# Sums of weight blocks moved from VectorE to GpSimd, and seven block products in ten gate and up units

## The chip, the cores and the metric

The kernel runs on one core of a Trainium2 chip. The metric is the device time of one execution in microseconds. Engines: TensorE (PE) multiplies matrices, VectorE (DVE) and ScalarE (ACT) work element by element, GpSimd (POOL) likewise, SyncE (SP) issues the loads.

## What is computed

One decoder layer on 256 tokens of width 2048, in fp32: a convolution group and an attention group, their mix, and a gated feed-forward network. The change is in the network alone:

```python
hf = rmsnorm(x, pre_ffn_norm[l])
ff = (jax.nn.silu(hf @ w_gate[l]) * (hf @ w_up[l])) @ w_down[l]
x = x + rmsnorm(ff, post_ffn_norm[l])
```

`w_gate` and `w_up` are 2048 x 5632, `w_down` is 5632 x 2048.

## The kernel before, in words

**Precision.** Every fp32 operand is split into two fp16 halves, and a product of two operands is three matmuls: high by high (L739), high by low (L740), low by high (L741). Activations are split once. Weights arrive as fp32 in a staging tile `st` (128 x 2048, 1 MB), ScalarE writes the high half `whi` (L694), VectorE the low half `wlo` from `st` and `whi` (L695).

**Pairs and units.** Weights are cut into pairs. A pair is two tiles of 128 rows by two groups of 512 columns, four blocks of 128 x 512 side by side in one staging tile. With two tiles of 128 tokens that is a product of 2 x 2 blocks by 2 x 2 blocks. `Unit.plain_all` does it with eight block products (24 matmuls). `Unit.fast` does it with seven (21 matmuls), from four further blocks that are sums of the weight blocks and from sums of the activation blocks. A gate and up unit is eight pairs and gives 512 gate and 512 up columns; there are eleven, `u` from 0 to 10. Of a gate and up unit's 512-column group half is gate and half is up; `swiglu` (L796, L806, and splits by L109) makes the network's hidden activations from it. Down has two units of 22 pairs, ten of them fast, in an order that alternates plain and fast and ends with two plain ones.

**A fast pair's weights.** `Feed.blocks` loads the pair, splits its first 1536 columns (three of the blocks) and then writes three sums over the staging tile in place, on VectorE at L709: one instruction of 2 x 512 columns and two of 512. `Feed.get` then splits all 2048 columns a second time, now of the four sums. A plain pair is split once, 2048 wide.

**What a fast unit adds at its end.** Four products have accumulators of their own in PSUM. After the last fast pair a ScalarE copy (L768), four adds on VectorE (L770 to L773) and four more in `block` (L782) put them together. Each of the eight adds has one input in PSUM. `hf_sums` (L669) makes the sums of the activations for gate and up in unit 0, `swiglu` those for down.

**What sets the order.** The program is written in the order in which TensorE uses the pairs: `get` issues pair `k` and pair `k + 1`. A scheduler then orders each engine's queue by that priority and by when inputs are ready, and inside the feed `chain` keeps an engine's instructions in the order written. Buffers limit how far it runs ahead: four staging tiles, eight `whi` and eight `wlo`. Each engine works off its queue strictly in order.

Of the kernel before, what the change touches and what calls it, by code (L numbers as in the profile page):

```python
# [10 lines left out]
F16 = mybir.dt.float16  # L11
F32 = mybir.dt.float32
I32 = mybir.dt.int32
AF = mybir.ActivationFunctionType
ALU = mybir.AluOpType
AX = mybir.AxisListType

P = 128
# [20 lines left out]

FAST = tuple(range(0, 20, 2))  # L40
NU = NG // 2
GU_UNITS = (1, 3, 5, 7, 9)
GU_FAST = 5
EPS = 1e-6
QK_SCALE = float((NOPE + ROPE) ** -0.5)
NEG = -1.0e30
# [14 lines left out]
def hymba_layer(ctx: ExitStack, tc: tile.TileContext, x, xT, pos, inv_freq, g_pre, w_in, w_lat,  # L61
                q_norm, w_uqn, w_uqp, kv_norm, w_uk, w_uv, conv_w, conv_v, g_attn,
                w_out, g_post, g_ffn, w_gu, w_dn, g_ffo, out):
    nc = tc.nc

    const = ctx.enter_context(tc.tile_pool(name="const", bufs=1))
    stage = ctx.enter_context(tc.tile_pool(name="stage", bufs=4))
    wsp = ctx.enter_context(tc.tile_pool(name="wsp", bufs=8))
    work = ctx.enter_context(tc.tile_pool(name="work", bufs=2))
    small = ctx.enter_context(tc.tile_pool(name="small", bufs=4))  # L70
# [3 lines left out]

    BF16 = mybir.dt.bfloat16
    KB = 256
    arena = const.tile([P, 82 * KB], F32, name="arena")

    def region(kb, shape, dtype=F32):

        n = int(np.prod(shape)) * (2 if dtype == F16 else 4) // 4
        a = int(kb * KB)
        v = arena[:, a : a + n]
        if dtype != F32:
            v = v.bitcast(dtype)
        names = "abcd"[: len(shape)]
        if len(shape) > 1:
            v = v.rearrange(f"p ({' '.join(names)}) -> p {' '.join(names)}", **dict(zip(names[:-1], shape[:-1])))
        return v
# [3 lines left out]
    def nm(base):  # L93
        uid[0] += 1
        return f"{base}_{uid[0]}"
# [20 lines left out]
    class Weights:  # L116


        def __init__(self, kt, n):
            self.kt, self.n = kt, n  # L120
            self.kpb = max(1, 2048 // n)
            self.parts = []
# [484 lines left out]
    for tb in range(NTB):  # L607
        ss4 = smalls(4)
        for j in range(4):
# [3 lines left out]
            m = mix[:, tb, cs]  # L613
# [31 lines left out]
    aw = region(44, (8, P))  # L645
    hw4 = region(48, (2, 4, P), F16)
    hw3 = region(50, (2, 3, P), F16)
    hS = region(70, (3, 16, P), F16)

    def a_of(k, tb):  # L650
        return aT[:, k // 2, 4 * tb + k % 2, :], aT[:, k // 2, 4 * tb + 2 + k % 2, :]
# [7 lines left out]
    def hf_fast(i):  # L659
        s = [(hS[:, i // 2, 2 * b + i % 2, :], hS[:, i // 2, 8 + 2 * b + i % 2, :]) for b in range(4)]  # L660
        return [hf_of(2 * i + 1, 1), hf_of(2 * i, 0), hf_of(2 * i + 1, 0), s[0], s[1], s[2], s[3]]

    def hf_sums(c):

        g0, g1 = [sized(tb, c).rearrange("p (i k t) -> p i k t", i=2, k=2) for tb in range(NTB)]
        sm = region(44, (4, 2, P))
        for d, p, m in ((0, g1[:, :, 0], g1[:, :, 1]), (1, g0[:, :, 0], g1[:, :, 0]),
                        (2, g0[:, :, 0], sm[:, 0]), (3, g0[:, :, 1], sm[:, 2])):
            nc.vector.tensor_tensor(sm[:, d], p, m, op=ALU.subtract)  # L669
        hl = region(48, (2, 8 * P), F16)  # L670
        split(hl[:, 0, :], hl[:, 1, :], sm.rearrange("p s i t -> p (s i t)"), X_S)
        nc.sync.dma_start_transpose(hS[:, c], hl.rearrange("p a n -> p (a n)"))

    class Feed:

        def __init__(self, pairs):
            self.pairs = pairs  # L680
            self.parts = {}
            self.st = {}
            self.last = {}

        def chain(self, engine, ins):
# [13 lines left out]
        def blocks(self, k):  # L699

            src, scale, fast = self.pairs[k]
            st = stage.tile([P, 2048], F32, tag="stage", name=nm("st")).rearrange("p (b n) -> p b n", b=4)
            nc.sync.dma_start(st, src)
            self.parts[k] = self.split(st, 1536 if fast else 2048, scale)
            if fast:
                b12 = st[:, 3:4, :].to_broadcast([P, 2, 512])
                for d, p, m in ((st[:, 0:4:3, :], st[:, 0:2, :], b12), (st[:, 1, :], st[:, 0, :], st[:, 1, :]),
                                (st[:, 2, :], st[:, 1, :], st[:, 2, :])):
                    self.chain("DVE", nc.vector.tensor_tensor(d, p, m, op=ALU.add))  # L709
                self.st[k] = st  # L710

        def get(self, k, ahead=1):
            for n in range(k, min(k + ahead + 1, len(self.pairs))):
                if n not in self.parts:
                    self.blocks(n)
            parts = self.parts[k]
            if k in self.st:
                parts = parts + self.split(self.st.pop(k), 2048, self.pairs[k][1])
            return parts

    class Unit:

# [31 lines left out]
        def fast(self, blocks, w, last):  # L754
            if self.sums is None:
                self.sums = [self.other() for _ in range(4)]
            X, Y, Z, Q = self.sums
            A22, A11, A12, S1, S3, S2, S4 = blocks
            self.mm(self.E[0][0], (0, 0), A12, w[2])
            self.mm(self.E[0][1], (0, 1), S4, w[1])  # L760
            self.mm(X, "X", A11, w[0], last)
            self.mm(Y, "Y", S2, w[4], last)
            self.mm(Z, "Z", S3, w[6], last)
            self.mm(Q, "Q", S1, w[3], last)
            self.mm(self.E[1][0], (1, 0), A22, w[5])
            if last:
                xs_ = work.tile([P, 512], F32, tag="hl", name=nm("xs"))
                nc.scalar.copy(xs_, X)  # L768
                m, n_, q2 = [work.tile([P, 512], F32, tag="ss", name=nm(b), bufs=3) for b in ("m", "n", "q2")]
                nc.vector.tensor_tensor(m, xs_, Y, op=ALU.subtract)  # L770
                nc.vector.tensor_tensor(n_, m, Z, op=ALU.add)
                nc.vector.tensor_tensor(m, Q, m, op=ALU.subtract)
                nc.vector.tensor_tensor(q2, Q, n_, op=ALU.subtract)  # L773
                self.fix = [[xs_, m], [n_, q2]]
# [10 lines left out]
    def swiglu(j, unit, c):  # L785
# [19 lines left out]
        for d, p, m in ((4, 0, 1), (5, 2, 0), (6, 2, 4), (7, 3, 6)):  # L805
# [5 lines left out]


    KP = KD // 2
    gu_order = [GU_FAST, 0, 1, GU_FAST + 1] + list(range(2, GU_FAST)) + list(range(GU_FAST + 2, KP))
    gu_orders = [gu_order if u in GU_UNITS else list(range(KP)) for u in range(NU)]

    slow = [i for i in range(NG) if i not in FAST]
    order = [i for f, p in zip(FAST, slow) for i in (p, f)] + slow[len(FAST) :]
    feed = Feed([(w_gu[u, i], W_S, u in GU_UNITS and i < GU_FAST) for u in range(NU) for i in gu_orders[u]]
                + [(w_dn[u, i], WD_S, i in FAST) for u in range(2) for i in order])  # L820
    for u in range(NU):
        unit = Unit(hf_of)
        if u == 0:
            ws = [feed.get(i, 0) for i in range(KP)]
            for tb in range(NTB):
# [3 lines left out]
                if tb == 0:  # L829
                    for c in range((GU_FAST + 1) // 2):  # L830
                        hf_sums(c)
        else:
            for n, i in enumerate(gu_orders[u]):
                w = feed.get(u * KP + n)
                if u in GU_UNITS and i < GU_FAST:
                    unit.fast(hf_fast(i), w, i == GU_FAST - 1)
                else:
# [150 lines left out]
```

## Time and profile before

| | |
|---|---|
| median of three runs | 1000.91 us (1000.34 to 1001.33) |
| the profiled execution | 1001.55 us |
| its span from the first to the last instruction | 999.7 us |
| TensorE busy | 959.6 us, 96% |
| VectorE busy | 876.3 us, 88% |
| ScalarE busy | 578.1 us, 58% |
| GpSimd busy | 33.6 us, 3% |
| gate and up: first matmul, then down | from 326 us; from 776 to 989 us |

The profiled execution is one run of the program with the hardware's profiler on; its span leaves out 1.85 us around the instructions. Busy time of TensorE counts overlapping matmuls once, so 96% says that it rarely stood still, not that it could do no more. Names such as `wlo<-st,whi` read: output from inputs. Times in rows are microseconds from the start of the span, "mean ns" are nanoseconds.

### The profile page before, as it was taken

What the parts mean: (1) busy time and instruction counts of PE and PEld (TensorE: products, weight loads), DVE (VectorE), ACT (ScalarE), POOL (GpSimd) and SP (SyncE); (2) the same over time, 40 slices, a digit from 0 to 9 for tenths busy, and PEclk for the clock granted to TensorE, in tenths of its full rate; (3) what the DMA queues carried; (4) which work ended last, traced back from release to release, by engine and by line L of the source; (5) the groups of instructions that cost most, each with busy time, mean ns of one, the idle gap of its engine ahead of it and who ended that gap; (6) DMA issues with size and microseconds to landing.
All of it is one profiled execution on the core that took longest, in us unless ns stands there. A gap on an engine that the chain in (4) does not pass through costs nothing.

```text
span 999.7 us, 11980 instructions
## 1 busy us (share of the span) xinstructions
PE 959.6 (96%) x4577; PEld 454.4 (45%) x4577; DVE 876.3 (88%) x1024; ACT 578.1 (58%) x632; POOL 33.6 (3%) x50
## 2 busy tenths in 40 slices
PE   6999997999899998999999999999999999999995
PEld 2444553775444443444444444444444444444442
DVE  6799999999967999989898997897996988899855
ACT  7796764664666555655656645654663565555521
POOL 0000000033100100000000000000000000000000
PEclk9999998999999999999999999999999999999998
DMA  8974656476654966776875874784686646645532
GB/s 340 346 262 126 243 197 192 154 247 211 211 210 118 325 167 197 256 278 197 320 214 178 317 236 155 272 288 156 220 309 234 218 185 246 238 175 220 210 127 85
DMA packets 84010, 221.95 MB, mean 222 GB/s; under 512 B 55792, under 2 KB 56432, under 8 KB 61424
## 3 DMA queue, kind: packets, MB, share of 16 engines
q1 hardware_dynamic: 83232, 220.26, 63.7%
q10 hardware_dynamic: 720, 0.93, 0.3%
q8 instruction: 36, 0.59, 0.2%
q14 instruction: 22, 0.18, 0.1%
HBM read 204.25 MB, written 4.19 MB: 209 GB/s over the span
## 4 chain that ended last, share of the span: by engine, by line
PE 60%; DVE 23%; issue 5%; ACT 4%; DMA 3%; POOL 1%; SPq 0%; DVEq 0%; POOLq 0%; ACTq 0%
PE acc L740 10%; PE acc L741 10%; PE acc L739 10%; PE tmp L741 6%; PE tmp L740 6%; PE tmp L739 6%; DVE wlo L695 6%; DVE arena L289 3%; DVE wlo L109 3%; DVE st L709 2%; PE acc L155 2%; PE acc L153 2%; PE acc L154 2%; DMA st<-in_w_gu 2%; POOL sm L207 1%
## 5 line engine op out<-in xcount | busy, mean ns | idle before, releaser
L694 ACT ACTIVATE whi<-st 128x2048 f16<-128x2048 f32 (+1 forms) x177 | 317.1, 1798 | 228.7 <-PE acc L741 77.6
L695 DVE SCALAR_TENSOR_TENSOR wlo<-st,whi 128x2048 f16<-128x2048 f32 (+1 forms) x177 | 375.2, 2150 | 52.9 <-ACT whi L694 52.5
L740 PE MATMUL acc<-wlo,arena 128*128 128x512 f16 x620 | 235.0, 379 | 4.7 <-DVE wlo L695 4.7
L739 PE MATMUL acc<-whi,arena 128*128 128x512 f16 x620 | 235.0, 379 | 2.5 <-DVE q L773 1.4
L741 PE MATMUL acc<-whi,arena 128*128 128x512 f16 x620 | 235.0, 379 | 0.0
L153 PE MATMUL acc<-whi,arena 128*128 128x512 f16 (+1 forms) x380 | 143.5, 378 | 5.5 <-ACT whi L108 5.5
L741 PEld LDWEIGHTS <-arena 128*128 128x128 f16 x951 | 93.0, 98 | 117.4 <-issue 5.6
L154 PE MATMUL acc<-wlo,arena 128*128 128x512 f16 (+1 forms) x380 | 143.4, 377 | 2.2 <-DVE wlo L109 2.0
L740 PEld LDWEIGHTS <-arena 128*128 128x128 f16 x951 | 93.0, 98 | 114.3 <-issue 2.4
L739 PEld LDWEIGHTS <-arena 128*128 128x128 f16 x951 | 93.0, 98 | 113.3 <-DVE a L796 1.2
L155 PE MATMUL acc<-whi,arena 128*128 128x512 f16 (+1 forms) x380 | 143.3, 378 | 0.0
L739 PE MATMUL tmp<-whi,arena 128*128 128x512 f16 x331 | 125.4, 379 | 0.0
L740 PE MATMUL tmp<-wlo,arena 128*128 128x512 f16 x331 | 125.4, 379 | 0.0
L741 PE MATMUL tmp<-whi,arena 128*128 128x512 f16 x331 | 125.4, 379 | 0.0
L109 DVE SCALAR_TENSOR_TENSOR wlo<-st,whi 128x2048 f16<-128x2048 f32 (+4 forms) x59 | 118.2, 2009 | 6.5 <-ACT whi L108 6.5
L709 DVE TENSOR_TENSOR st<-st 128x1024 f32<-128x1024 f32 x135 | 117.2, 868 | 4.1
L108 ACT ACTIVATE whi<-st 128x2048 f16<-128x2048 f32 (+4 forms) x59 | 98.5, 1677 | 34.4 <-PE acc L155 10.3
L289 DVE SCALAR_TENSOR_TENSOR arena<-arena 128x256 f32<-128x256 f32 x184 | 78.5, 488 | 0.0
L153 PEld LDWEIGHTS <-arena 128*128 128x128 f16 x380 | 37.8, 99 | 47.4 <-ACT arena L113 5.0
L155 PEld LDWEIGHTS <-arena 128*128 128x128 f16 x380 | 37.8, 99 | 44.8 <-issue 5.1
L154 PEld LDWEIGHTS <-arena 128*128 128x128 f16 x380 | 37.6, 99 | 42.3 <-issue 2.8
L295 ACT ACTIVATE x_sb<-arena 128x256 f32<-128x256 f32 x56 | 25.3, 506 | 10.1 <-DVE arena L297 10.1
(209 smaller groups left out, 667.9 us busy)
## 6 DMA issues: line engine op xcount, KB each, us to landing
st<-in_w_gu SPq DMA_DIRECT2D x88, 1024.0 KB, 5.5
st<-in_w_dn SPq DMA_DIRECT2D x44, 1024.0 KB, 5.0
st<-in_w_out SPq DMA_DIRECT2D x16, 1024.0 KB, 5.1
st<-in_w_in SPq DMA_DIRECT2D x14, 1024.0 KB, 9.2
st<-in_w_lat SPq DMA_DIRECT2D x12, 896.0 KB, 5.5
x_sb<-in_x SPq DMA_DIRECT2D x4, 1024.0 KB, 8.6
st<-in_w_uqn SPq DMA_DIRECT2D x4, 768.0 KB, 4.9
st<-in_w_uv SPq DMA_DIRECT2D x2, 1024.0 KB, 5.9
```

The costliest lines, as they stand in the source:

```text
L108: nc.scalar.activation(hi, src, AF.Copy, scale=scale)
L109: nc.vector.scalar_tensor_tensor(lo, src, scale, hi, op0=ALU.mult, op1=ALU.subtract)
L153: nc.tensor.matmul(p_ap, xh, wh, start=(start and k == 0), stop=False)
L154: nc.tensor.matmul(p_ap, xh, wl, start=False, stop=False)
L155: nc.tensor.matmul(p_ap, xl, wh, start=False, stop=(stop and k == wgt.kt - 1))
L289: nc.vector.scalar_tensor_tensor(cacc[:, cb, :], upad[:, cb, k : k + S], cw[:, cb, k : k + 1], cacc[:, cb, :], op0=ALU.mult, op1=ALU.add)
L694: self.chain("ACT", nc.scalar.activation(hi[:, :n], src, AF.Copy, scale=scale))
L695: self.chain("DVE", nc.vector.scalar_tensor_tensor(lo[:, :n], src, scale, hi[:, :n], op0=ALU.mult, op1=ALU.subtract))
L709: self.chain("DVE", nc.vector.tensor_tensor(d, p, m, op=ALU.add))
L739: nc.tensor.matmul(ps, ah, bh, start=key not in self.begun, stop=False)
L740: nc.tensor.matmul(ps, ah, bl, start=False, stop=False)
L741: nc.tensor.matmul(ps, al, bh, start=False, stop=last)
```

## The change

The three sums of a fast pair go from VectorE to GpSimd. Fast pairs are now in gate and up units 1 to 10 instead of 1, 3, 5, 7 and 9, four in each instead of five: 40 instead of 25. Down keeps its 20. A fifth staging tile is added, for which the arena gives up 6 KB per partition; two groups of activation sums are made instead of three. The feed issues up to four pairs ahead instead of one, and the second splits one pair ahead.

```diff
-GU_UNITS = (1, 3, 5, 7, 9)
-GU_FAST = 5
+GU_UNITS = tuple(range(1, NU))
+GU_FAST = 4
+
+AHEAD, AHEAD_T = 4, 1
...
-    stage = ctx.enter_context(tc.tile_pool(name="stage", bufs=4))
+    stage = ctx.enter_context(tc.tile_pool(name="stage", bufs=5))
...
-    arena = const.tile([P, 82 * KB], F32, name="arena")
+    arena = const.tile([P, 76 * KB], F32, name="arena")
...
-    hS = region(70, (3, 16, P), F16)
+    hS = region(68, (2, 16, P), F16)
...
-            self.parts = {}
-            self.st = {}
+            self.parts, self.sums, self.st = {}, {}, {}
...
-                    self.chain("DVE", nc.vector.tensor_tensor(d, p, m, op=ALU.add))
+                    self.chain("POOL", nc.gpsimd.tensor_tensor(d, p, m, op=ALU.add))
                 self.st[k] = st
 
-        def get(self, k, ahead=1):
+        def get(self, k, ahead=AHEAD):
             for n in range(k, min(k + ahead + 1, len(self.pairs))):
                 if n not in self.parts:
                     self.blocks(n)
-            parts = self.parts[k]
-            if k in self.st:
-                parts = parts + self.split(self.st.pop(k), 2048, self.pairs[k][1])
-            return parts
+            for n in range(k, min(k + AHEAD_T + 1, len(self.pairs))):
+                if n in self.st:
+                    self.sums[n] = self.split(self.st.pop(n), 2048, self.pairs[n][1])
+            return self.parts[k] + self.sums.get(k, [])
...
-    gu_order = [GU_FAST, 0, 1, GU_FAST + 1] + list(range(2, GU_FAST)) + list(range(GU_FAST + 2, KP))
+    gu_order = [4, 0, 5, 1, 6, 2, 3, 7]
```

VectorE's queue before, at the first two fast pairs of a gate and up unit (`st` is a staging tile, its number the tile's own):

```order
L695 SCALAR_TENSOR_TENSOR wlo_3861<-st_3858,whi_3860 128x1536
L709 TENSOR_TENSOR st_3858<-st_3858 128x2x512
L709 TENSOR_TENSOR st_3858<-st_3858 128x512 x2
L695 SCALAR_TENSOR_TENSOR wlo_3894<-st_3891,whi_3893 128x1536
L709 TENSOR_TENSOR st_3891<-st_3891 128x2x512
L709 TENSOR_TENSOR st_3891<-st_3891 128x512 x2
L695 SCALAR_TENSOR_TENSOR wlo_3901<-st_3858,whi_3900 128x2048
```

Each first split is followed by its three sums. VectorE's queue after the change, over the middle of a gate and up unit:

```order
L695 SCALAR_TENSOR_TENSOR wlo_4039<-st_3934,whi_4038 128x2048
L695 SCALAR_TENSOR_TENSOR wlo_4069<-st_4066,whi_4068 128x1536
L695 SCALAR_TENSOR_TENSOR wlo_4076<-st_3968,whi_4075 128x2048
L695 SCALAR_TENSOR_TENSOR wlo_4103<-st_4100,whi_4102 128x2048
L695 SCALAR_TENSOR_TENSOR wlo_4139<-st_4136,whi_4138 128x1536
L695 SCALAR_TENSOR_TENSOR wlo_4212<-st_4209,whi_4211 128x2048
L770 TENSOR_TENSOR m_4129<-xs_4127,acc_3944 128x512
L695 SCALAR_TENSOR_TENSOR wlo_4216<-st_4066,whi_4215 128x2048
```

The sums are gone from it, and a tile's second split (of `st_4066`) stands six rows behind its first. GpSimd's queue after the change, for the tiles of the same unit:

```order
L709 TENSOR_TENSOR st_3934<-st_3934 128x512 x2
L709 TENSOR_TENSOR st_3968<-st_3968 128x2x512
L709 TENSOR_TENSOR st_3968<-st_3968 128x512 x2
L709 TENSOR_TENSOR st_4066<-st_4066 128x2x512
L709 TENSOR_TENSOR st_4066<-st_4066 128x512 x2
L709 TENSOR_TENSOR st_4136<-st_4136 128x2x512
```

Sixty such triples stand there, one behind the other, with nothing else between them.

## Rows read from the trace of the kernel before

**Rows 1.** The page, busy time, share and instructions of each engine.
```profile
PE 959.6 (96%) x4577; PEld 454.4 (45%) x4577; DVE 876.3 (88%) x1024; ACT 578.1 (58%) x632; POOL 33.6 (3%) x50
```

**Rows 2.** Busy time by stretch, gate, up and down; the first line names the columns.
```profile
core 0: us, PE busy (x) PEld busy (x) DVE busy (x) ACT busy (x) POOL busy (x), PEclk, DMA share, GB/s
...
370.00:408.00 38.00, 34.79 (x161) 15.47 (x159) 36.39 (x35) 21.30 (x18) 0.00 (x0) 1.00 0.66 211
408.00:449.00 41.00, 41.00 (x192) 18.57 (x191) 36.16 (x37) 24.28 (x22) 0.00 (x0) 1.00 0.75 263
...
609.00:776.00 167.00, 167.00 (x776) 75.73 (x774) 145.08 (x144) 94.94 (x84) 0.00 (x0) 1.00 0.67 233
776.00:883.00 107.00, 107.00 (x498) 48.48 (x497) 95.83 (x72) 58.61 (x41) 0.00 (x0) 1.00 0.57 208
...
326.00:989.00 663.00, 655.73 (x3036) 296.71 (x3034) 586.76 (x545) 360.25 (x299) 4.04 (x3) 1.00 0.65 224
```

**Rows 3.** TensorE's waits: for whom, us in total, times, longest.
```profile
PE tmp L385 <- DVE kp L384: 6.2, 1, 6.2
...
PE acc L740 <- DVE wlo L695: 4.7, 3, 2.2
```

**Rows 4.** Timeline of GpSimd, attention: start, us, line, operation, tiles, count.
```profile
226.32 0.73 POOL L500 TENSOR_TENSOR arena<-arena,sq 128x256 f32<-128x256 f32 x1 [3.63 <-ACT sq L496]
...
232.65 0.75 POOL L500 TENSOR_TENSOR arena<-arena,sq 128x256 f32<-128x256 f32 x1 [4.34 <-ACT sq L496]
...
240.23 1.81 POOL L500 TENSOR_TENSOR arena<-arena,sq 128x256 f32<-128x256 f32 x1 [2.66 <-ACT sq L496]
...
245.98 0.82 POOL L500 TENSOR_TENSOR arena<-arena,sq 128x256 f32<-128x256 f32 x1 [2.70 <-ACT sq L496]
```

**Rows 5.** Timeline of VectorE at the same moments, and three conv adds at 200.92.
```profile
200.92 1.27 DVE L289 SCALAR_TENSOR_TENSOR arena<-arena 128x256 f32<-128x256 f32 x3
...
226.57 0.48 DVE L114 SCALAR_TENSOR_TENSOR arena<-tmp,gat,arena 128x256 f16<-128x256 f32 x1 [1.22 <-ACT arena L113]
...
232.72 2.82 DVE L109 SCALAR_TENSOR_TENSOR wlo<-st,whi 128x2048 f16<-128x2048 f32 x1
...
239.17 2.28 DVE L109 SCALAR_TENSOR_TENSOR wlo<-st,whi 128x2048 f16<-128x2048 f32 x1
241.37 0.47 DVE L114 SCALAR_TENSOR_TENSOR arena<-tmp,gat,arena 128x256 f16<-128x256 f32 x1
...
245.35 2.53 DVE L289 SCALAR_TENSOR_TENSOR arena<-arena 128x256 f32<-128x256 f32 x5
```

**Rows 6.** Timeline of VectorE, the fix-ups and `swiglu` of gate and up unit 1.
```profile
410.34 0.68 DVE L770 TENSOR_TENSOR m<-xs,acc 128x512 f32<-128x512 f32 x1
...
417.40 2.28 DVE L695 SCALAR_TENSOR_TENSOR wlo<-st,whi 128x2048 f16<-128x2048 f32 x1
419.60 1.15 DVE L109 SCALAR_TENSOR_TENSOR arena<-arena 128x512 f16<-128x512 f32 x2
...
421.40 2.28 DVE L695 SCALAR_TENSOR_TENSOR wlo<-st,whi 128x2048 f16<-128x2048 f32 x1
423.60 0.42 DVE L109 SCALAR_TENSOR_TENSOR ahl<-a,ahl 128x256 f16<-128x256 f32 x1
```

**Rows 7.** Groups by line and shape, the first split of fast pairs; busy, mean ns.
```profile
L695 DVE SCALAR_TENSOR_TENSOR wlo<-st,whi 128x1536 f16<-128x1536 f32 x45 | 78.8, 1751 | 10.6 <-ACT whi L694 10.6
```

**Rows 8.** Timeline of VectorE, down: three sums, then the splits behind them.
```profile
788.90 2.68 DVE L709 TENSOR_TENSOR st<-st 128x1024 f32<-128x1024 f32 x3
791.50 6.16 DVE L695 SCALAR_TENSOR_TENSOR wlo<-st,whi 128x2048 f16<-128x2048 f32 x3
```

**Rows 9.** Loads: count, KB each, median us from issue to landing.
```profile
st<-in_w_gu SPq DMA_DIRECT2D x88, 1024.0 KB, 5.5
```

**Rows 10.** Busy time by stretch, behind TensorE's wait of 6.2 us (columns as in rows 2).
```profile
160.00:170.00 10.00, 7.37 (x22) 3.08 (x23) 8.87 (x26) 5.67 (x11) 1.17 (x2) 0.66 0.51 135
```

## Prediction

> **What bounds the kernel now.** Read four views in this order. First the page's engine totals [rows 1]: TensorE is busy for 96% of the span and VectorE for 88%, so two engines stand close to the end, and the question is which of them sets it in the part that is edited. Second, the busy time by stretch [rows 2], cut at the edges of the gate and up units. Between 326 and 989 us TensorE runs for 655.73 of 663 us; in the 167 us from 609 to 776 it issues 776 matmuls, one each 0.215 us, with no gap. The same rows give VectorE's load: 36.39 of 38 us in a unit with fast pairs (370 to 408), 36.16 of 41 in the plain unit after it, 145.08 of 167 further on, 95.83 of 107 in the first half of the down projection. ScalarE has 360.25 of 663, GpSimd 4.04. Third, TensorE's waits [rows 3]: the largest in this part is for a low half that VectorE writes, 4.7 us in 3 waits. So **TensorE bounds gate, up and down, VectorE follows some 10% behind it**, and GpSimd is free. Fourth, since the change loads GpSimd, GpSimd and VectorE side by side in the attention part, the only place where both work on SBUF at once [rows 4, 5].
>
> **The change part by part.**
>
> *Matmuls.* A pair is 24 matmuls plain and 21 fast. Five units of 5 fast and 3 plain pairs (177) and six plain units (192) were 2037; ten units of 4 and 4 (180) and one plain unit are 1992. That is 45 fewer, at 0.215 us each 9.7 us of TensorE time. It is a gain only if TensorE still sets the pace. A unit then needs 180 x 0.215 = 38.7 us of TensorE.
>
> *Splits and fix-ups on VectorE.* There are 40 fast pairs in gate and up instead of 25, and each needs a second split. A 2048-wide split starts the next instruction after 2.20 us (417.40 to 419.60 in [rows 6]), a 1536-wide one after 1.75 - 0.08 = 1.67 us ([rows 7]; 0.08 is the overlap that the 2048 form has, 2.28 busy against 2.20). So each new unit has 8 x 2.20 + 4 x 1.67 = 24.3 us of splits. The eight fix-up adds and the gate's own work behind them took 410.34 to 417.40, 419.60 to 421.40 and 0.42 us in unit 1 [rows 6], together 9.3 us; the adds now come in ten units. VectorE's own time per unit is thus 24.3 + 9.3 = **33.6 us**, under the 38.7 of TensorE. Of that the eight adds (0.68 busy, so 0.60 each, 4.8 us) read an accumulator in PSUM and one tile in SBUF; the other 28.8 us read two tiles from SBUF.
>
> *The sums.* The three adds per fast pair took 2.60 us on VectorE (788.90 to 791.50 in [rows 8]); 60 pairs now do them on GpSimd. The trace has no such add there, but it has a two-input add of 256 columns [rows 4]. Free, it takes 0.73 us (226.32, while VectorE reads PSUM). The three cover 1024 + 512 + 512 columns, eight times as many, so 5.8 us if everything scales. What matters is what it does to VectorE, and [rows 4, 5] show it four times. At 232.65 GpSimd starts an add, VectorE starts a 2048-wide split 0.07 us later, and the split takes 2.82 us where it takes 2.28 otherwise (239.17): 0.54 us late. At 240.23 the order is the other way, VectorE is inside a split that ends at about 241.4, and the add of 0.73 us takes 1.81. At 245.98 five conv adds on VectorE take 2.53 us instead of the 2.08 that five would (three take 1.27 at 200.92, so 0.40 each and the overlap). At 226.32, where VectorE's instruction (226.57, 0.48 us) has one input in PSUM, neither is delayed. **I read this as mutual exclusion: a GpSimd add and a VectorE instruction with two SBUF inputs do not run together, so their times add up.** I price a triple at the time it blocks VectorE, 0.54 x 8 = 4.3 us, because that row is the same operation and the same data type. The upper end is 5.8 (all of the busy time blocks), the lower end 2.60 (GpSimd as fast as VectorE; the 0.73 us against at most 0.48 for VectorE's 256-column instructions excludes better).
>
> [...]
>
> *Gate and up.* Per unit, VectorE's 33.6 plus GpSimd's 4 x 4.3 = 17.2, less what stands beside the PSUM adds. The order puts one triple in four (that of the fast pair whose first split precedes the fix-up) next to them; I credit 2 us. That is **48.8 us per unit against 38.7 of TensorE**, so VectorE and GpSimd together become the bound. Units 1 to 10 took 370 to 776 us, 40.6 each. +8.2 x 10 = **+82 us**. The 9.7 us of saved matmuls vanish in TensorE's new waits.
>
> *Down.* Twenty times a plain and a fast pair: VectorE 2.20 + 1.67 + 2.20 = 6.1 and GpSimd 4.3, 10.4 us against 45 x 0.215 = 9.7. +0.7 x 20 = 14, and some 4 us where the fix-ups of the first half fall into a queue that has no slack left: **+18 us**. Before, these sums cost VectorE 2.6 and left it 1.0 us of slack per period.
>
> *What I cost at nothing.* ScalarE's 15 more splits and 5 more copies (about 25 us over 663) lie in its 300 idle us [rows 2]. The third group of activation sums that falls away in unit 0 saves some 4 us of VectorE there; unit 0 then ends with VectorE no further ahead than before. The fifth staging buffer and the deeper prefetch take latency away: a load lands in 5.5 us [rows 9], under the time of two pairs, and a staging buffer that waits for GpSimd is the reason for the fifth. Were it missing, loads would queue behind the second split; with it nothing is saved, since loads did not hold TensorE. SP's queue carries the same number of weight loads. The new waits: ScalarE's second split of a fast pair waits for GpSimd's triple, with the next pairs' high halves queued behind it, and VectorE waits for those. The order puts five or six VectorE rows between a first split and its second, some 10 us or more, so a triple of 4.3 us, each add behind at most one split of 2.2 us, is done about in time; I add nothing, and its cost would show as VectorE pausing for ScalarE. GpSimd's own queue holds only triples there.
>
> Sum: 1001.55 + 82 + 18 = 1101.5 for the execution that was profiled (span 999.7 and 1.85 around it); it lies 0.6 above the median of the three runs, so I predict **1100 us**.
>
> **The rivals.**
>
> *TensorE stays the bound, and it is faster.* GpSimd's adds would have to slip in beside VectorE's splits. Then 9.7 us go, and part of the 7.3 us of TensorE's gaps between 326 and 989 [rows 2]: 990 us. For it: VectorE alone has 33.6 of 38.7 us, GpSimd about 23 of 38.7. It decides at the price of a triple: once it blocks VectorE for less than (38.7 - 33.6 + 2) / 4 = 1.8 us, TensorE leads again. It would take a long add that gives way to VectorE in the middle, where the 256-column one did not. [...] Chance 0.12.
>
> *No change.* A triple that blocks for about 2.3 us gives units of 40.6 us. This needs GpSimd faster than VectorE's own 2.60, and [rows 4] speak against it. Chance 0.03.
>
> *Much slower.* If all 5.8 us of a triple block, a unit is 33.6 + 23.2 - 2 = 54.8 us, +142, and a down period 11.9, +44 and 4: 1191 us. A second push in the same direction is the TensorE clock: after a wait of 6.2 us [rows 3] it was granted 0.66 of full speed over the 10 us that followed [rows 10], and the new waits are some 10 us per unit. At half speed TensorE loses a few us per wait, which its 10 us of slack should absorb. Chance of over 1160: 0.03.
>
> *Slower, but by less than my range.* A triple of 2.6 to 3.2 us would give 1016 to 1040: 33.6 + 10.4 - 2 = 42.0 us per unit at the lower end, +14, and nothing in down. Chance 0.02.
>
> **How the numbers follow.** The forecast, both engines sharing one path, has 0.80, and with the two cases beside it slower has 0.85. A triple of 3.2 us gives units of 44.4 and +38, with the down periods at 9.3 hidden under TensorE and 4 us for the fix-ups, some 1043; one of 5.3 us gives 52.8 (+122), down +34 and 4, some 1161. The range is **1040 to 1160**, which leaves out the fast rival, the tie and the outer ends. Chances by 0.2% (2 us, about what a measurement of this kernel can tell): faster 0.12, same 0.03, slower 0.85.
>
> **What would show it.** Right: GpSimd's adds take well over 5.8 us per triple with their waiting; the 2048-wide splits have a mean clearly above 2.29 us, some of them 4 us and more (1024-column adds in front); VectorE and GpSimd busy without a pause from 370 us on; TensorE with some 10 us of waits per unit, for low halves; units of about 49 us. Wrong: splits at 2.28 us beside a busy GpSimd, units of 39 us, TensorE without gaps. If the units come out right but down does not, the price of a triple is right and the slack of down was misjudged; if the splits are stretched but units stay near 41 us, the adds found more room beside PSUM work than I credit.

## The result, and the profile after

The changed kernel takes **1099.44 us** (median of 4 runs, 1098.99 to 1100.22) against 1001.08 us of the kernel before in the same comparison: ratio 1.0985, 95% interval 1.0966 to 1.1004. It is slower by 98.4 us; 1100 was predicted. The profiled execution of the changed kernel has a span of 1097.3 us, that of before 999.7, so 97.6 us are to be found.

The page after, engine totals, which answer to [rows 1]:

```profile
PE 982.0 (89%) x4532; PEld 457.5 (42%) x4532; DVE 980.5 (89%) x937; ACT 597.5 (54%) x651; POOL 615.5 (56%) x230
```

VectorE has 87 instructions fewer and is busy 104 us longer; GpSimd went from 33.6 to 615.5 us. TensorE issues 45 matmuls fewer and yet is busy 22 us longer. The chain that ended last, by engine:

```profile
DVE 42%; issue 17%; POOL 17%; PE 13%; ACT 5%; DMA 1%; DVEq 0%; POOLq 0%; ACTq 0%
```

VectorE and GpSimd hold 59% of it, TensorE 13%. Where the time sits is read from three edges: the first gate matmul (row of line 739: count, then duration, then first and last start), units 1 to 10, and down. Before:

```profile
L739 PE MATMUL acc<-whi,arena x620: 376/379/389, 326.5 to 988.7; 128*128 128x512 f16 x155
...
370.30:774.20 403.90, 398.85 (x1846) 180.34 (x1845) 361.44 (x349) 229.16 (x196) 0.00 (x0) 1.00 0.69 238
774.20:881.70 107.50, 107.50 (x500) 48.74 (x499) 96.22 (x77) 59.11 (x45) 0.00 (x0) 1.00 0.58 210
881.70:989.10 107.40, 107.40 (x499) 48.69 (x498) 85.89 (x69) 48.53 (x34) 0.54 (x1) 1.00 0.45 169
```

After (the windows have the columns of [rows 2]; 617.60 to 665.60 is one unit of the steady part, 908.80 to 919.20 one down period):

```profile
L739 PE MATMUL acc<-whi,arena x500: 376/379/634, 336.0 to 1086.3; 128*128 128x512 f16 x167
...
379.80:857.70 477.90, 410.14 (x1801) 179.46 (x1800) 434.65 (x312) 247.53 (x211) 383.07 (x121) 0.96 0.57 195
617.60:665.60 48.00, 39.62 (x181) 17.61 (x180) 43.50 (x33) 24.60 (x22) 38.29 (x13) 1.00 0.57 191
857.70:973.50 115.80, 110.12 (x500) 48.94 (x499) 110.29 (x54) 57.21 (x41) 96.74 (x31) 0.99 0.58 205
973.50:1086.70 113.20, 108.54 (x500) 48.60 (x498) 103.81 (x50) 49.24 (x39) 87.53 (x28) 1.00 0.46 160
908.80:919.20 10.40, 9.94 (x47) 4.45 (x46) 10.40 (x4) 5.09 (x3) 10.24 (x4) 1.00 0.58 204
```

By stage: gate starts 9.5 us later (326.5 to 336.0), the ten units take 74.0 us more (403.9 to 477.9, now 47.8 each), down 14.1 more (214.9 to 229.0); together 97.6. In the steady unit VectorE is busy for 43.50 and GpSimd for 38.29 of 48.00 us. Those two can't be added: an add that is held up counts as busy while it stands (11.69 us for one of 2.35, in a row further down). The groups by shape show both engines stretched; the second row answers to [rows 7] with its 1751 ns:

```profile
L695 DVE SCALAR_TENSOR_TENSOR wlo<-st,whi 128x2048 f16<-128x2048 f32 x132 | 380.8, 2920 | 47.2 <-ACT whi L694 47.2
L695 DVE SCALAR_TENSOR_TENSOR wlo<-st,whi 128x1536 f16<-128x1536 f32 x60 | 148.1, 2469 | 5.5 <-ACT whi L694 5.2
...
L709 POOL TENSOR_TENSOR st<-st 128x512 f32<-128x512 f32 x120 | 288.4, 2404 | 9.4
L709 POOL TENSOR_TENSOR st<-st 128x1024 f32<-128x1024 f32 x60 | 287.0, 4784 | 124.6 <-DVE wlo L695 78.1 <-issue 35.1 <-ACT whi L694 7.2
```

A split that nothing disturbs still takes 2.28 us (2048) or 1.74 (1536); 67 of the 132 and 34 of the 60 are longer, up to 4.46 and 3.9. An undisturbed add takes 2.35 us (1024 columns) or 1.26 (512), so a triple 4.87; with its waiting it takes 4.78 + 2 x 2.40 = 9.6. What an add costs a split is seen best in down, where VectorE does nothing else; one period, three splits back to back:

```profile
909.52 2.81 DVE L695 SCALAR_TENSOR_TENSOR wlo<-st,whi 128x1536 f16<-128x1536 f32 x1
912.26 3.35 DVE L695 SCALAR_TENSOR_TENSOR wlo<-st,whi 128x2048 f16<-128x2048 f32 x1
915.53 4.45 DVE L695 SCALAR_TENSOR_TENSOR wlo<-st,whi 128x2048 f16<-128x2048 f32 x1
```

Two adds of 512 columns (from 907.53 and 910.80 us) and one of 1024 (from 913.42) run in turn with them, and the splits take 1.07, 1.07 and 2.17 us longer than undisturbed. The opposite case is an add beside VectorE instructions that read PSUM, in gate and up; neither side is held up (0.68 us as in [rows 6], 1.27 against 1.26 undisturbed):

```profile
431.53 0.68 DVE L772 TENSOR_TENSOR m<-acc,m 128x512 f32<-128x512 f32 x1
432.12 0.68 DVE L773 TENSOR_TENSOR q<-acc,n 128x512 f32<-128x512 f32 x1
...
431.62 1.27 POOL L709 TENSOR_TENSOR st<-st 128x512 f32<-128x512 f32 x1
```

What waits for what (us in total, times, longest):

```profile
ACT whi L694 <- POOL st L709: 160.3, 37, 7.2
...
DVE wlo L695 <- ACT whi L694: 52.3, 18, 4.5
...
PE tmp L740 <- DVE wlo L695: 25.1, 16, 2.4
PE acc L740 <- DVE wlo L695: 21.9, 14, 2.4
```

ScalarE's second splits wait 160 us for the sums (36.9 in the kernel before, where VectorE made them), and TensorE 47 us for low halves, against 4.7 in [rows 3]. VectorE waits 52 us for ScalarE; it did so for 52.5 before, but there TensorE set the pace and waited for low halves for 4.7 us only. The engine keeps the order of its queue meanwhile: the eight instructions of VectorE's queue after the change, printed above, start one after the other from 452.83 to 474.62 us, with 4.45 us of waiting among them.

### The profile page after: what moved, and what is told of

Its sections match the earlier page's. It is cut to its first block, busy times and chain, and to the rows that moved or that the text cites. A ratio compares the mean times of both kernels' runs of the same rounds, so it can differ in the third digit from the quotient of the medians.

```text
span 1097.3 us, 12125 instructions
## 1 busy us (share of the span) xinstructions
PE 982.0 (89%) x4532; PEld 457.5 (42%) x4532; DVE 980.5 (89%) x937; ACT 597.5 (54%) x651; POOL 615.5 (56%) x230
## 4 chain that ended last, share of the span: by engine, by line
DVE 42%; issue 17%; POOL 17%; PE 13%; ACT 5%; DMA 1%; DVEq 0%; POOLq 0%; ACTq 0%
DVE wlo L695 20%; POOL st L709 15%; DVE arena L291 4%; DVE arena L806 3%; DVE a L796 3%; ACT whi L694 3%; DVE wlo L111 2%; PE acc L157 2%; PE acc L156 2%; PE acc L155 2%; DVE arena L299 1%; PE acc L464 1%; POOL ss L483 1%; POOL sm L209 1%; DVE arena L111 1%
## 5 line engine op out<-in xcount | busy, mean ns | idle before, releaser
L709 POOL TENSOR_TENSOR st<-st 128x1024 f32<-128x1024 f32 x180 | 574.5, 3197 | 134.0 <-DVE wlo L695 78.1
L695 DVE SCALAR_TENSOR_TENSOR wlo<-st,whi 128x2048 f16<-128x2048 f32 (+1 forms) x192 | 524.7, 2779 | 52.6 <-ACT whi L694 52.3
L694 ACT ACTIVATE whi<-st 128x2048 f16<-128x2048 f32 (+1 forms) x192 | 330.6, 1767 | 215.4 <-POOL st L709 160.3
L740 PE MATMUL acc<-wlo,arena 128*128 128x512 f16 x500 | 192.7, 385 | 19.4 <-DVE wlo L695 19.4
L739 PE MATMUL acc<-whi,arena 128*128 128x512 f16 x500 | 192.2, 384 | 17.9 <-DVE n L771 9.6
L741 PE MATMUL acc<-whi,arena 128*128 128x512 f16 x500 | 192.5, 385 | 0.0
L740 PE MATMUL tmp<-wlo,arena 128*128 128x512 f16 x436 | 168.8, 387 | 20.6 <-DVE wlo L695 20.6
L739 PE MATMUL tmp<-whi,arena 128*128 128x512 f16 x436 | 168.7, 387 | 15.2 <-DVE n L771 11.3
L741 PE MATMUL tmp<-whi,arena 128*128 128x512 f16 x436 | 168.5, 386 | 0.0
L740 PEld LDWEIGHTS <-arena 128*128 128x128 f16 x936 | 92.7, 99 | 152.1 <-issue 47.8
L209 POOL TENSOR_TENSOR sm<-sm,neg_half 128x1 f32<-128x1 f32 (+1 forms) x12 | 13.7, 1141 | 251.6 <-DVE sm L207 251.6
```

What stands on the lines that cost most here:

```text
L694: self.chain("ACT", nc.scalar.activation(hi[:, :n], src, AF.Copy, scale=scale))
L695: self.chain("DVE", nc.vector.scalar_tensor_tensor(lo[:, :n], src, scale, hi[:, :n], op0=ALU.mult, op1=ALU.subtract))
L709: self.chain("POOL", nc.gpsimd.tensor_tensor(d, p, m, op=ALU.add))
L739: nc.tensor.matmul(ps, ah, bh, start=key not in self.begun, stop=False)
L740: nc.tensor.matmul(ps, ah, bl, start=False, stop=False)
L741: nc.tensor.matmul(ps, al, bh, start=False, stop=last)
```

## The experiments

Four theories stand in what was expected. A: an add on GpSimd and a split on VectorE exclude each other, so their times add up. B: they don't, and a triple only comes late for those who read it. C: the fifth staging tile delays the attention part. D: something else in the new order does that. Each kernel was timed beside the kernel before on the same chip.

**The sums back on VectorE, all else as changed.**

```diff
-                    self.chain("POOL", nc.gpsimd.tensor_tensor(d, p, m, op=ALU.add))
+                    self.chain("DVE", nc.vector.tensor_tensor(d, p, m, op=ALU.add))
```

> The changed kernel with its three sums back on VectorE, all else as changed. Theory A (VectorE and GpSimd exclude each other, their times add up): VectorE alone then carries 33.6 + 4 x 2.6 = 44.0 us per gate and up unit instead of the 48.1 that the changed kernel shows, -41 us over ten units, and in down 8.7 us per plain and fast pair lie under TensorE's 9.7 again, -18: some 1040 us. Theory B (nothing excludes, GpSimd's triple only comes late for the second split): the late triples are gone, VectorE's 44.0 us per unit bound it as well, 1040 us. The two agree here; the run prices the move by itself.

1042.44 us, ratio 1.0411 (1.0380 to 1.0442). The ten units:

```profile
381.30:812.60 431.30, 399.73 (x1802) 176.59 (x1801) 425.24 (x429) 240.97 (x205) 0.00 (x0) 0.99 0.63 211
```

43.1 us per unit, VectorE busy for 42.5 of them. So of the 98 us, some 57 come from where the sums are done. The rest is there with GpSimd idle: 40 fast pairs are more than VectorE can split and sum in TensorE's time (38.9 us per unit in the kernel without sums, below), and the first gate matmul again comes late, at 337.5 us.

**The kernel before, its sums on GpSimd.**

```diff
-                    self.chain("DVE", nc.vector.tensor_tensor(d, p, m, op=ALU.add))
+                    self.chain("POOL", nc.gpsimd.tensor_tensor(d, p, m, op=ALU.add))
```

> The kernel before with its sums on GpSimd and nothing else changed (five of eight pairs in five units, four staging tiles, one pair ahead). Theory A: a fast unit has 35.3 us of VectorE and 5 x 4.9 of GpSimd, 59.8 less some 2 beside PSUM work, against 38.1 of TensorE; the plain unit next to it has 19 us of VectorE slack, of which the short lead can use about half, so +8 to +12 per fast unit, +50, and down +18: 1060 to 1080 us. Theory B: VectorE is relieved by 2.6 us per pair, only the chain to the second split is longer; with one pair ahead up to 5 us per fast unit: 1000 to 1025 us.

1081.48 us, ratio 1.0803 (1.0777 to 1.0829): a little above A's range, far above B's. But the waits and the window over down show that A is not all of it here:

```profile
ACT whi L694 <- POOL st L709: 268.8, 40, 8.3
...
DVE wlo L695 <- ACT whi L694: 217.5, 61, 6.9
...
812.30:1069.20 256.90, 228.01 (x997) 99.55 (x995) 143.55 (x93) 104.20 (x76) 122.20 (x55) 0.95 0.45 159
```

In down VectorE is busy for 143.55 of 256.90 us and for the rest waits for ScalarE's high halves. With one pair of lead the chain add, second high half, second low half is itself the limit. In the changed kernel, with four pairs of lead and a fifth tile, VectorE waits for ScalarE for 9.4 us of down and 52.3 in all.

**Adds that nobody reads.** They write to a spare tile, and the second split takes the raw blocks.

```diff
+                scr = region(40 if k < NU * KP else 68, (2, 512))
...
-                    self.chain("POOL", nc.gpsimd.tensor_tensor(d, p, m, op=ALU.add))
+                    self.chain("POOL", nc.gpsimd.tensor_tensor(scr if d.shape[1] == 2 else scr[:, 0], p, m, op=ALU.add))
```

> The changed kernel with GpSimd's adds writing to a spare tile that nobody reads; the second split takes the blocks as loaded (so the sums are left out of the result). The adds still read the staging tiles. No one waits for a triple any more but the next load of its tile. Theory A: the same times still add up, units near 48 us less what the waits for late triples cost, 1070 to 1100 us. Theory B: the chain is cut, TensorE bounds with 38.7 us per unit: 990 us.

1082.45 us, ratio 1.0822 (1.0794 to 1.0851), so A. The totals, the wide splits, and the ten units:

```profile
PE 977.6 (91%) x4532; PEld 457.0 (42%) x4532; DVE 1003.1 (93%) x937; ACT 599.6 (56%) x651; POOL 552.3 (51%) x230
...
L695 DVE SCALAR_TENSOR_TENSOR wlo<-st,whi 128x2048 f16<-128x2048 f32 x132 | 382.0, 2930 | 1.2 <-ACT whi L694 1.2
...
388.70:842.10 453.40, 407.22 (x1802) 179.40 (x1801) 447.68 (x311) 244.87 (x207) 317.90 (x118) 0.97 0.60 204
```

Neither ScalarE nor VectorE waits for the adds any more (the 47.2 us in front of the wide splits are 1.2), and the wide splits are as long as in the changed kernel, 2.93 us. So cutting the chain gives back 17 of the 98 us; the rest stays. By stage it isn't so plain: the units take 45.3 us each, 2.4 less than in the changed kernel, and VectorE is busy for 447.68 of their 453.40 us, but unit 0 in front of them takes 54.2 us in place of 43.8, with one wait of 10.5 us for a low half. Unit 0, here and then in the changed kernel:

```profile
334.50:388.70 54.20, 43.71 (x194) 19.32 (x193) 52.62 (x47) 25.81 (x31) 23.29 (x11) 0.91 0.73 230
```

```profile
336.00:379.80 43.80, 41.63 (x194) 18.84 (x193) 42.26 (x46) 22.89 (x28) 11.19 (x5) 1.00 0.85 269
```

Eleven adds already run there in place of five, and VectorE is busy for 10.4 us more: part of the exclusion has only moved forward.

**No sums at all.**

```diff
-                for d, p, m in ((st[:, 0:4:3, :], st[:, 0:2, :], b12), (st[:, 1, :], st[:, 0, :], st[:, 1, :]),
-                                (st[:, 2, :], st[:, 1, :], st[:, 2, :])):
-                    self.chain("POOL", nc.gpsimd.tensor_tensor(d, p, m, op=ALU.add))
```

> The changed kernel without the adds; the second split takes the blocks as loaded (the sums are left out of the result). VectorE has 33.6 us per unit, TensorE 38.7. Both theories: TensorE bounds, 45 matmuls fewer than before (-9.7 us) and part of the 7.3 us of gaps: 986 to 992 us. [...]

995.90 us, ratio 0.9961 (0.9946 to 0.9976).

```profile
380.60:769.40 388.80, 388.80 (x1803) 176.29 (x1802) 334.69 (x319) 247.82 (x208) 0.00 (x0) 1.00 0.72 242
```

The units are TensorE's own, 38.9 us each without a gap; VectorE works for 33.5 of them (33.6 was predicted). Down takes 107.5 and 107.3 us, as before. The total is 4 us above the expected range because the first gate matmul comes at 336.8 us, so the late start has nothing to do with GpSimd's adds.

**Half of each add** (256 of 512 columns).

```diff
+                    self.chain("POOL", nc.gpsimd.tensor_tensor(d[..., :256], p[..., :256], m[..., :256], op=ALU.add))
```

> The changed kernel with each of GpSimd's adds on half its columns (256 in place of 512; the other half of the sums is left out of the result). An undisturbed triple of the changed kernel is 2.35 + 2 x 1.26 = 4.9 us, so some 2.7 us now. Theory A as a sum: 33.6 + 4 x 2.7 = 44.4 us per unit, less some 4 to 5 beside VectorE's PSUM adds, 39.5 to 40.5 against 38.7 of TensorE; down 6.1 + 2.7 = 8.8 under 9.7, so back to 107.4 per half; the attention part 9.5 later than before: 1000 to 1020 us. If the loss were set by late starts of the adds (behind VectorE's splits) and not by their length, half of it or more would stay: above 1040 us.

1011.18 us, ratio 1.0103 (1.0089 to 1.0117).

```profile
377.90:782.40 404.50, 393.86 (x1801) 175.86 (x1800) 366.53 (x313) 243.53 (x208) 279.84 (x121) 1.00 0.67 229
```

40.45 us per unit, 1.6 above TensorE's 38.9 of the kernel without sums: VectorE's 33.5 and half of 17.3 are 42.2, less 1.7 beside PSUM work. The cost follows the columns that GpSimd adds.

**Low halves from one input** (a scaled copy in place of the split).

```diff
-            self.chain("DVE", nc.vector.scalar_tensor_tensor(lo[:, :n], src, scale, hi[:, :n],
-                                                             op0=ALU.mult, op1=ALU.subtract))
+            self.chain("DVE", nc.vector.tensor_scalar(lo[:, :n], src, scale, None, op0=ALU.mult))
```

> The changed kernel with VectorE's low split replaced by an instruction that reads the staging tile alone (a scaled copy to fp16; the low halves are left out of the result). Theory A, narrow (only instructions with two SBUF inputs exclude GpSimd's adds): no split is stretched beside an add, TensorE bounds, 990 to 1002 us. Theory A, wide (a VectorE instruction that streams fp32 from SBUF at double rate excludes them as well): a split takes about 1.2 us alone and is stretched by 1 to 2.3 us where an add runs; 24.3 us of splits become some 13, VectorE's 22 plus GpSimd's 19.5 is 42 per unit against 38.7 of TensorE: 1010 to 1040 us.

1038.62 us, ratio 1.0386 (1.0370 to 1.0401). The copy alone on VectorE, one beside adds, and those adds on GpSimd:

```profile
561.16 1.22 DVE L695 TENSOR_SCALAR wlo<-st 128x2048 f16<-128x2048 f32 x1
...
572.91 2.80 DVE L695 TENSOR_SCALAR wlo<-st 128x2048 f16<-128x2048 f32 x1 [1.23 <-PE tmp L739]
...
572.27 4.56 POOL L708 TENSOR_TENSOR st<-st 128x1024 f32<-128x1024 f32 x2 [14.04 <-ACT whi L694]
```

This copy is held up too, 2.80 us in place of 1.22 (the split of two inputs takes 2.28 for the same 2048 columns); the mean of the 132 wide ones is 1.77 us. So it does not take two SBUF inputs to collide. The total decides less: VectorE is far from full here, busy for 335.4 of the 433.5 us of the units, and the fix-ups come late (TensorE waits 30.2 us for them), so the 38 us were not followed further.

**Four staging tiles.**

```diff
-    stage = ctx.enter_context(tc.tile_pool(name="stage", bufs=5))
+    stage = ctx.enter_context(tc.tile_pool(name="stage", bufs=4))
```

> The changed kernel with four staging tiles instead of five, nothing else. The changed kernel reaches the first gate matmul at 336.0 us of its span, the kernel before at 326.5; the sums only begin after that. Theory C: the fifth tile lets a 2048-wide split of the mix weights run on VectorE in front of GpSimd's softmax scaling in heads 4 to 6 (1.3 us becomes 3.2), and TensorE waits for it: with four tiles the first gate matmul is back at 325 to 328 us. Rival D: something else in the program's order did it (the smaller arena, the third group of sums): it stays at 334 to 338. In gate, up and down four tiles are held longer by late triples, 0 to +20 us there: 1088 to 1110 us in all under C, 1098 to 1120 under D.

1106.43 us, ratio 1.1057 (1.1043 to 1.1071). The first gate matmul is back at 326.8 us, so it is the fifth tile that delays attention. How, is seen at GpSimd's softmax scaling (line 483), here and then in the changed kernel:

```profile
221.96 1.32 POOL L483 TENSOR_SCALAR ss<-ss,sm 128x128 f32<-128x128 f32 x2 [0.25 <-DVE sm L479]
```

```profile
221.97 3.31 POOL L483 TENSOR_SCALAR ss<-ss,sm 128x128 f32<-128x128 f32 x2
...
222.39 2.28 DVE L111 SCALAR_TENSOR_TENSOR wlo<-st,whi 128x2048 f16<-128x2048 f32 x1
...
220.00:230.00 10.00, 8.90 (x48) 6.67 (x47) 5.71 (x10) 2.10 (x7) 5.23 (x3) 0.83 0.63 210
```

With a tile more, the next `w_out` split is ready just then and runs into the scaling, which takes 3.31 us in place of 1.32; TensorE's waits for the scaling are 5.4 us between 195 and 260 us (1.0 in the kernel before), and its granted clock over these 10 us is 0.83 in the last row. The same happens at 211.19 and 232.50 us (3.19 and 3.25 us, against 1.39 and 1.28 in the kernel before), some 5.8 us for the three together, and the clock is 0.83 in each 10 us from 210 to 250 where it was 1.00 before. How the 9.5 us divide between scaling and clock was not separated. But the units take 49.4 us each without the fifth tile, and ScalarE waits 136.6 us for weight loads in place of 38.9, so the kernel is 7 us slower than the changed one.

**The fifth tile for gate, up and down only.**

```diff
+    stage5 = ctx.enter_context(tc.tile_pool(name="stage5", bufs=1))
...
+            pool = stage5 if k % 5 == 4 else stage
```

> The kernel after the change, with its fifth staging tile in a pool of its own that only gate, up and down use, for every fifth pair; attention keeps the four tiles of before. It computes all that the reference asks. By theory C (the fifth tile is what delays the attention part, since a split of mix or w_out weights then runs right in front of GpSimd's softmax scaling) the first gate matmul comes at 325 to 328 us as before instead of 336.0, and since five tiles still feed gate and up the rest stays as long as in the changed kernel: 1088 to 1092 us. By theory D (the order or the layout of the arena does it) the first gate matmul stays near 336 us and the time at 1098 to 1101 us. If the four-tile run's extra 16 us in gate and up came from an earlier start meeting later loads rather than from the missing tile, the start returns to 327 and the time to 1099 to 1107 us all the same.

1103.02 us, ratio 1.1029 (1.1005 to 1.1053): the third case. The first gate matmul is at 325.9 us, and the 10 us come back in the units:

```profile
371.40:859.40 488.00, 418.25 (x1802) 181.22 (x1801) 413.72 (x312) 243.60 (x208) 368.80 (x121) 0.95 0.56 190
```

488.0 us in place of 477.9, with VectorE busy for 413.7 in place of 434.7: between 326 and 860 us ScalarE waits 91.4 us for sums (74.7 in the changed kernel) and 56.4 for gate and up loads (38.9). So the late start is the fifth tile's doing, yet undoing it alone gains nothing. The two kernels also differ in the order of VectorE's queue: in the changed kernel the next first split stands directly behind the last fix-up add, as the first two rows show, in this one the gate's own work comes there (the other two):

```profile
434.31 0.68 DVE L782 TENSOR_TENSOR q<-tmp,q 128x512 f32<-128x512 f32 x1
434.91 1.75 DVE L695 SCALAR_TENSOR_TENSOR wlo<-st,whi 128x1536 f16<-128x1536 f32 x1
```

```profile
426.17 0.67 DVE L784 TENSOR_TENSOR q<-tmp,q 128x512 f32<-128x512 f32 x1
426.76 0.47 DVE L798 SCALAR_TENSOR_TENSOR arena<-n,r_f,sg 128x256 f32<-128x256 f32 x1
```

Whether this order costs the 10 us was not tested, so their cause stays open.

**Can anything of the change be kept?** Four kernels were built on the one before: the deeper lead alone; with a fifth tile for the feed-forward part only; that with six fast pairs per fast unit; and the softmax scaling on VectorE alone. The edits in turn:

```diff
+AHEAD, AHEAD_T = 4, 1
...
+            pool = stage5 if k % 5 == 4 else stage
...
-GU_FAST = 5
+GU_FAST = 6
...
-            nc.gpsimd.tensor_scalar(d, d, rc[:, qb : qb + 1], 0.0, op0=ALU.mult, op1=ALU.add)
+            nc.vector.tensor_scalar(d, d, rc[:, qb : qb + 1], None, op0=ALU.mult)
```

> The kernel before with the deeper issue order alone (up to four pairs ahead, second splits one ahead), four staging tiles, sums on VectorE. TensorE has 8 us of gaps in gate, up and down to lose and nothing else: 993 to 1001 us under either theory. If it is above 1005, the deeper lead itself costs, by splits that run before more urgent work.

1018.02 us, ratio 1.0175 (1.0162 to 1.0188), a miss. ScalarE waits 132.9 us for gate and up loads in place of 59.6, which fits a deeper lead that holds each of four tiles longer; the next run, with a fifth tile, is back at the time of before.

> As the last, with a fifth staging tile that only gate, up and down use, so that the attention part keeps four. Sums on VectorE, five of eight pairs in five units. 992 to 1000 us; the first gate matmul at 325 to 328 us under theory C of the run with four staging tiles, at 334 to 338 under D.

1001.16 us, ratio 1.0015 (1.0004 to 1.0025): no gain, and just outside the expected range. Gate starts at 327.0 us, and TensorE's waits for low halves are 7.6 us, against 4.7 before.

> The kernel with the fifth tile for gate, up and down alone, sums on VectorE, and six of eight pairs in the five units in place of five: 15 matmuls fewer, -3.2 us of TensorE. VectorE: a fast unit 6 x 6.5 + 2 x 2.2 + 9.3 = 52.7, the plain one 22, together 74.7 us against 78.7 of TensorE. If five tiles of lead carry the 14.7 us by which the fast unit falls behind, 996 to 1000 us; if not, TensorE waits up to 5 us per fast unit, 1005 to 1025.

1010.52 us, ratio 1.0095 (1.0081 to 1.0109), the second case: five tiles of lead do not carry what a fast unit falls behind, and TensorE's waits for low halves grow to 13.6 us.

> The kernel before with the softmax scaling of the eight heads (16 instructions of 128 or 256 columns) on VectorE in place of GpSimd. Under theory A each one on GpSimd delays or is delayed by VectorE's two-input work (0.2 to 2 us each in the trace of before, one of them of 2.26 us); on VectorE they take about 0.2 us each, 3 us in all, in a stretch where VectorE is 95% busy. Gain of 0 to 4 us: 996 to 1001 us. If the exclusion did not matter there, +0 to +3 us for VectorE's added work.

1001.17 us, ratio 1.0007 (0.9994 to 1.0019): nothing that can be measured. The only kernel clearly below the one before is the one that leaves the sums out.

## Why the prediction was right, and where it was not

*What binds, and the mechanism: right.* Mutual exclusion was read from four places in the trace and priced from one 2.82 us split. The longest split of the change takes 4.46 us, 2.18 above its own 2.28, about one undisturbed 1024-column add (2.35). Unread adds keep most of the loss, halved adds shrink it, no adds remove it. A rival that neither the prediction nor the theories name is that both run on side by side at a lower rate; the times would add up as well. The row of 11.69 us below speaks against it: four splits beside that add are not lengthened at all.

*The price of a triple: right, where nothing hides it.* 4.3 us was predicted. A down period leaves nothing to hide in and takes 10.40 us, as predicted: 10.40 less the splits' 6.07 is 4.33. That 0.54 us could be taken times eight is no luck: 256 columns cost a split 0.54 us there, 512 cost 1.07 and 1024 cost 2.17 here. Undisturbed, a triple takes 4.87.

*Gate and up: two terms mis-sized, in opposite directions.* +82 was predicted, +74.0 measured. VectorE's 33.6 us per unit is confirmed (33.5 without sums). I put 17.2 - 2 = 15.2 us of blocking on top and no waiting. The windows show 43.5 us of VectorE work per unit, so only 10.0 of blocking, and 4.3 of waiting for ScalarE's high halves, which wait for late sums. With unread adds it is 11.3 and 0.6. So four triples cost VectorE 10 to 11 us here and not 17: an add beside PSUM reads, as at 431.62 us, or beside a waiting VectorE holds nothing up. The credit of 2 us was some 4 to 5 too small, and the waiting gave most of that back.

*Down: slightly mis-sized.* +18 predicted, +14.1 measured. The 14 from the periods is all of it; the 4 us for fix-ups did not come.

*"What I cost at nothing": two steps failed.* First, the fifth staging buffer. I wrote that it only takes latency away; it also brings a split forward into the attention part, where GpSimd's scaling is on TensorE's path, and gate starts 9.5 us later. The rows that I used to price the adds [rows 4, 5] are of that very part, and I did not ask what an earlier load would trigger there. Second, "each add behind at most one split of 2.2 us". This is what happened once, on GpSimd and then on VectorE:

```profile
445.64 11.69 POOL L709 TENSOR_TENSOR st<-st 128x1024 f32<-128x1024 f32 x1 [3.49 <-DVE wlo L695]
...
446.23 8.89 DVE L695 SCALAR_TENSOR_TENSOR wlo<-st,whi 128x2048 f16<-128x2048 f32 x4
```

One add stands for 11.69 us while four splits run back to back, undelayed. So ScalarE waits 160 us for sums, and lateness, which I set at nothing, is worth 17 us of the total, as the run with unread adds shows.

*Why the total fits all the same.* The start that I missed (9.5) met units that came out 8 lower than I put them and a down part 4 lower; in the units themselves, lateness that I left out met a credit that I set too small. That 1099 and 1100 agree to a tenth of a per cent is in part luck. Two runs show besides that these terms are not independent: with the fifth tile kept from attention the 10 us that the start gains are lost in the units, and with unread adds 10 us of the 24 that the units gain are lost again in unit 0.

*The rivals.* TensorE as the bound needed a triple that blocks for under 1.8 us; it blocked for 4.33 in down and, at 10.0 us for four, for 2.5 in gate and up. Beside the adds the two-input splits (up to 4.46 us against 2.28) and the one-input copy (2.80 against 1.22) are both stretched. The case of all 5.8 us blocking fell too, since an undisturbed triple takes only 4.87. Its second push, TensorE's clock (0.50 granted from 162 to 168 us in the kernel before), shows as 0.96 granted over the units, and 1800 matmuls are busy 410 us in place of 387; the steady unit at 1.00 is as long as the mean, so this sets nothing.

*What was to be seen.* Triples over 5.8 us with waiting (9.6), wide splits clearly over 2.29 (2.92, the longest 4.46), units of about 49 us (47.8), TensorE some 10 us per unit off its pace (47.8 - 38.7 = 9.1): all there. "VectorE and GpSimd busy without a pause" was not: in the ten units VectorE stands still for 43 of 478 us, waiting for ScalarE.

## What to carry to other kernels

Before moving work to GpSimd to relieve VectorE, look in the trace for one moment where both work on SBUF, and read which of the two got longer: if they exclude each other, the move adds GpSimd's longer time (here up to 4.33 us for a triple) in place of VectorE's shorter one (2.60), and only what falls beside PSUM reads or a waiting VectorE is free (beside PSUM reads 512 columns took 1.27 us here, 1.26 undisturbed). A row of totals with a free GpSimd (3%) says nothing about that. And a buffer more is not free because it removes a wait: ask which instruction it lets start earlier, and whose path that lies on.

## What the runs showed of the hardware that was not expected

- GpSimd was kept out while VectorE ran four splits back to back: 11.69 us for an add that takes 2.35 alone. In down, with splits just as close, one add got in at every split, and in the attention part one between five back-to-back conv adds (the last row of [rows 4]). What decides which comes first stays open.
- What an add costs a split goes with the add's columns and is a little under the add's own time: 1.07 us for 512 (1.26 undisturbed), 2.17 for 1024 (2.35).
- A single-input fp32 to fp16 copy on VectorE, 1.22 us for 2048 columns alone, collides as well: 2.80 us beside two adds, 1.77 in the mean of 132.
- A short GpSimd instruction with one wide input, the softmax scaling, is held up by a split as an add is: two of them took 3.31 us in place of 1.32.
